# First norm of a two-layer decoder kernel: weight and shift applied behind the transposes

## The chip, the cores and the metric

The kernel runs on one core of one Trainium2 chip. The metric is the device time of one execution in microseconds (us). Engines: PE is TensorE (matmuls and transposes), DVE is VectorE, ACT is ScalarE, POOL is GpSimd, SP is SyncE, which here only issues DMAs. Each engine runs its instructions in order and waits for others by semaphores.

## The reference

Input x is 512 tokens of 2048 channels, float32. Layer 0 is a state-space mixer, layer 1 sparse attention with 16 heads; behind each a norm of the residual sum:

```
y = s5_mixer(x, ...)                       # layer 0, ends in "@ w_out" (1024 x 2048)
x1 = layer_norm(alpha * x + y, g0, b0)     # (v - mean) * rsqrt(var + eps) * g0 + b0
shared = shared_kv(x1, ...)                # x1 @ kv_w, block compression of K and V
y = nsa_mixer(x1, w_in, w_out, shared)     # x1 @ w_in: queries, gates
out = layer_norm(alpha * x1 + y, g1, b1)
```

Mean and variance run over the 2048 channels of a token; g and b are vectors over the channels. x1 has two uses: transposed (channels on the partitions) as an operand of all of layer 1's projections, and as it is, in the residual sum at the very end.

## The kernel before

A float32 product is made of three fp32r matmuls (`mm3`, L233 to L237): every operand is kept as a high part h, rounded by a copy on ACT, and a low part l, the difference, made by DVE. Below, a "product" is one such triple. Weights come in units of 128 x 1024: `Weights` loads a unit by SP (L56), splits it on ACT (L78) and DVE, or POOL for the units in `pool_units` (L85), two units ahead of use; `ahead(i)` forces the splits up to unit i. Split units lie in three buffers ("hl"); `W.extra` gives some units another pool and tag.

`project_out` (L904) does the last projection of a layer, the residual sum and the norm. Tokens lie on the partitions: four token tiles t of 128, four channel stretches cc of 512. The last of its four steps goes tile by tile, eight products a tile, and at each tile's end `done` adds the residual into v (L951), takes statistics (L952) and starts `finish(t)`. `finish` is a generator: it issues a piece of the norm of its tile, yields a number, and `Background.tick` continues it when that many ticks have gone by; a full product counts 3 ticks, a half product of layer 1's first tiles 1.5, so 21 ticks are 7 and 14 products. Its pieces stand in the engines' queues between the products of the next tiles. Lanes are served in the order of the tiles, and per tick one or two are continued.

For the first norm (`turn` is true) `finish` takes mean and variance (L962) and the root (L964, ACT), then subtracts the mean and multiplies with g (L970, DVE) for some stretches, makes the inverse of the root (L975 to L980), and then, by the letters in `LN_HOW`, multiplies with it and adds b: "d" on DVE (L983), "m" on ACT and POOL (L985, L986), "p" wholly on ACT and POOL (L988 to L990). The tile is then stored to x1_d for the residual (L1004, SP) and turned: four transposes per stretch on PE into a PSUM tile tp (two buffers, L1010), a copy from it to the high part (ACT, L1012), a subtraction from it to the low part (DVE, L1014). The low part reads tp, so tp is free only behind it.

After the last tile come the first two projection tiles of layer 1 (unit u1 to u1+3, split on POOL), in two halves of 256 tokens, 32 half products each: half 0 needs tiles 0 and 1 turned, half 1 tiles 2 and 3. `layer1_in` does the rest: its products tick a second `Background`, which holds the compression of K and V and the attention heads. POOL has, in the order of issue, small loads (`pos`, `w2`, L1181, L1185) and a memset of `ct` (L1240) that the compression waits for on ACT; its last small projection, `p`, is on PE. Before the first head, `bg.drain()` runs all that is left in the background, and the memory of this phase's pool is given to the heads.

The lines around the change:

Of the kernel before, what the change touches and what calls it, by code (L numbers as in the profile page):

```python
# [21 lines left out]
D = 2048  # L22
KD = D // 128
# [9 lines left out]
LN_EPS = 1e-5  # L33
# [130 lines left out]
def emit(tc, A, out):  # L164
# [34 lines left out]
    with ExitStack() as top:  # L199
        const = top.enter_context(tc.tile_pool(name="const", reuse_waits="tile", bufs=1))  # L200
        wp = top.enter_context(tc.tile_pool(name="wp", reuse_waits="tile", bufs=1))
        xp = top.enter_context(tc.tile_pool(name="xp", reuse_waits="tile", bufs=1))
        dram = top.enter_context(tc.tile_pool(name="dram", bufs=1, space=DRAM))
        W = Weights(nc, wp, units)
        W.by_dma.update(range(DMA_FROM, index["w_glu", 0]))
        c = Core(tc, A, W, index, const, xp)
        c.scope, c.dram = top, dram
        sz_d = dram.tile([KE, 128, T], F32, name="sz_d")
        x1_d = dram.tile([4, 128, D], F32, name="x1_d")
        y_d = dram.tile([NH, 128, T], F32, name="y_d")  # L210

        with ExitStack() as sc:
            yh, yl, yscope = layer0_in(c, sc, sz_d)
        with yscope, ExitStack() as sc:
            xh, xl = project_out(c, sc, index["w_out"], OUT0, KE, yh, yl, lambda k: None, A["x"], A["ln_g"][0],
                                 A["ln_b"][0], x1_d, True)
        with ExitStack() as sc:
            y = layer1_in(c, sc, seq, xh, xl, y_d)
# [685 lines left out]
def project_out(c, sc, u0, steps, K, yh, yl, prep, x_res, ln_g, ln_b, x_out, turn):  # L904
# [10 lines left out]
    n_u = K // 2  # L915
# [43 lines left out]
    fg = FG[turn]  # L959

    def finish(t):
# [3 lines left out]
        vs, gs, bs = ([z[:, cc * 512:cc * 512 + 512] for cc in range(4)] for z in (v[:, t], gb, bb))  # L965
        how = LN_HOW[turn][t]
        late = []
        early = [cc for cc in range(4) if how[cc] != "p"]
        for i, cc in enumerate(early):
            V.scalar_tensor_tensor(vs[cc], vs[cc], mv[:, t, 0:1], gs[cc], OP.subtract, OP.mult)  # L970
            if i % 2:
                yield fg[0]
            if i == (len(early) - 1 if turn else 1):

                V.reciprocal(r, r)  # L975
                V.tensor_scalar(q, mv[:, t, 1:2], LN_EPS, r, OP.add, OP.mult)
                V.tensor_scalar(q, q, r, -0.5, OP.mult, OP.mult)
                V.tensor_scalar(r, q, 1.5, r, OP.add, OP.mult)
                if "p" in how:
                    V.tensor_scalar(nb, mv[:, t, 0:1], r, -1.0, OP.mult, OP.mult)  # L980
        for cc in sorted(range(4), key=lambda cc: "pmd".index(how[cc])):
            if how[cc] == "d":
                V.scalar_tensor_tensor(vs[cc], vs[cc], r, bs[cc], OP.mult, OP.add)  # L983
            elif how[cc] == "m":
                S.activation(vs[cc], vs[cc], AF.Copy, scale=r)  # L985
                P.tensor_tensor(vs[cc], vs[cc], bs[cc], OP.add)  # L986
            else:
                S.activation(vs[cc], vs[cc], AF.Identity, scale=r, bias=nb)  # L988
                P.tensor_tensor(vs[cc], vs[cc], gs[cc], OP.mult)
                P.tensor_tensor(vs[cc], vs[cc], bs[cc], OP.add)  # L990
            if not turn:
                o = x_out[t, :, cc * 512:cc * 512 + 512]
                if how[cc] == "d":
                    SP.dma_start(o, vs[cc])
                elif POUT:
                    P.dma_start(o, vs[cc])
                else:
                    late.append((o, vs[cc]))
            yield fg[1]
        if not turn:  # L1000
            for o, z in late:
                SP.dma_start(o, z)
            return
        SP.dma_start(x_out[t], v[:, t])  # L1004
        yield fg[2]
        ts = slice(t * 128, t * 128 + 128)
        for cc in range(4):
            tp = pt.tile([128, 4, 128], F32, name="tp")
            for i in range(4):
                PE.transpose(tp[:, i], vs[cc][:, i * 128:i * 128 + 128], ident)  # L1010
            h, l = (z[:, 4 * cc:4 * cc + 4, ts] for z in (xh, xl))
            S.copy(h, tp)  # L1012
            yield fg[3]
            V.tensor_tensor(l, tp, h.bitcast(F32), OP.subtract)  # L1014
            turned[t] += 1

    bg = Background(4, True)

    def done(cc, t, ps):
        add(cc, t, ps)  # L1020
        if cc == 3:
            bg.add(t, finish(t))
            bg.advance(t)

    for step, (cc, tiles) in enumerate(steps):
# [55 lines left out]
POUT = 0

FG = {True: (9, 1, 9, 6), False: (4, 3)}

LN_HOW = {True: ('pddp', 'dppd', 'mdmm', 'dmmm'), False: ('dddd', 'dddd', 'dddd', 'dddd')}
# [395 lines left out]
SCALE = 128.0 ** -0.5  # L1481


def layer1_in(c, sc, seq, xh, xl, y_d):
# [170 lines left out]
```

## Time and profile before

| | |
|---|---|
| median of 3 runs | 1802.88 us (1795.56 to 1807.08) |
| profiled execution | 1799.01 us, span 1797.0 us |
| PE busy | 1742.9 us, 97% of the span |
| DVE busy | 1005.1 us, 56% |
| ACT busy | 607.3 us, 34% |
| POOL busy | 177.5 us, 10% |
| chain that ended last | PE 81%, DVE 3%, ACT 1% |
| mean granted clock of PE | 0.993 |

The profile is of one execution, whose own time stands beside its span; the runs of the table are others. Busy time is that of an engine's instructions; where PE is busy throughout, the other engines' work lies beside it and costs nothing. The chain is followed back from the last instruction, at each step to what released it. [...]

### The profile page before, as it was taken

The numbers are of one execution on the slowest core, as the hardware profiler recorded it, in microseconds if no ns is written. First come the engines' busy times: TensorE is split into PE (matmuls) and PEld (weight loads), VectorE is DVE, ScalarE is ACT, GpSimd is POOL, SyncE is SP. The second block draws the span as 40 slices with busy tenths as digits, with TensorE's granted clock in tenths as the row PEclk, the third lists the DMA queues.
The fourth block names the chain that finished last, engine by engine and source line by source line (L and its number), as shares of the span: only waits on it lengthen the run. The fifth ranks groups of instructions, "written<-read, shape, count | busy, mean of one in ns | idle before, by whom it ended". The sixth has DMA issues, their size and how long they took to land.

```text
span 1797.0 us, 21851 instructions
## 1 busy us (share of the span) xinstructions
PE 1742.9 (97%) x8455; PEld 1446.2 (80%) x8455; DVE 1005.1 (56%) x1817; ACT 607.3 (34%) x1020; POOL 177.5 (10%) x233
## 2 busy tenths in 40 slices
PE   8799999997999999999999999999999999999997
PEld 6678887886788888888888888888888888888886
DVE  7678866458233455653555553555543555665346
ACT  3344435324333333332323332333332333333120
POOL 4911100006000000000000000000000000010000
PEclk9999999999999999999999999999999999999999
DMA  6587874543233322222222222222222222236343
GB/s 226 139 198 195 215 173 146 192 148 141 83 118 117 106 83 77 82 83 83 89 78 81 88 79 92 88 76 88 76 84 94 88 77 82 77 129 232 120 140 105
DMA packets 89751, 209.70 MB, mean 117 GB/s; under 512 B 25264, under 2 KB 34720, under 8 KB 88624
## 3 DMA queue, kind: packets, MB, share of 16 engines
q1 hardware_dynamic: 81008, 181.31, 30.5%
q0 software_dynamic: 6336, 22.81, 5.2%
q10 hardware_dynamic: 2304, 4.20, 0.6%
q8 instruction: 66, 1.08, 0.2%
q14 instruction: 37, 0.30, 0.0%
HBM read 188.42 MB, written 19.86 MB: 116 GB/s over the span
## 4 chain that ended last, share of the span: by engine, by line
PE 81%; DVE 3%; ACT 1%; issue 0%; DMA 0%; POOL 0%; SPq 0%; DVEq 0%; POOLq 0%; ACTq 0%
PE ps L235 23%; PE ps L237 23%; PE ps L236 23%; PE tp L1459 2%; PE s L237 1%; PE s L235 1%; PE s L236 1%; PE o L236 1%; PE o L237 1%; DVE v L970 1%; PE o L235 1%; PE cps L1224 1%; PE tp L1424 0%; PE tp L1010 0%; DMA z<-sz_d 0%
## 5 line engine op out<-in xcount | busy, mean ns | idle before, releaser
L235 PE MATMUL ps<-x1h,hl 128*128 128x512 f32 (+1 forms) x1440 | 564.8, 392 | 1.6 <-ACT hl L78 1.6
L237 PE MATMUL ps<-x1h,hl 128*128 128x512 f32 (+1 forms) x1440 | 557.9, 387 | 0.5 <-DVE hl L85 0.5
L236 PE MATMUL ps<-x1l,hl 128*128 128x512 f32 (+1 forms) x1440 | 556.8, 387 | 0.0
L85 DVE TENSOR_TENSOR hl<-wr,hl 128x1024 fp32r<-128x1024 f32 (+1 forms) x247 | 300.9, 1222 | 311.3 <-ACT hl L78 307.4
L78 ACT CAST hl<-wr 128x1024 fp32r<-128x1024 f32 (+1 forms) x273 | 284.4, 1045 | 223.3 <-PE ps L237 183.6
L237 PEld LDWEIGHTS ps<-x1h,hl 128*128 128x128 f32 x1440 | 271.4, 189 | 57.3 <-DVE hl L85 1.0
L235 PEld LDWEIGHTS ps<-x1h,hl 128*128 128x128 f32 x1440 | 272.0, 189 | 48.5 <-ACT hl L78 1.8
L236 PEld LDWEIGHTS ps<-x1l,hl 128*128 128x128 f32 x1440 | 271.9, 189 | 46.6
L1396 ACT ACTIVATE p<-s,m 128x384 f32<-128x384 f32 (+3 forms) x128 | 67.7, 529 | 357.9 <-DVE m L1395 357.9
L1332 POOL TENSOR_TENSOR y<-y,z 128x512 f32<-128x512 f32 x32 | 41.5, 1298 | 999.8 <-DVE z L1331 863.0
L241 DVE TENSOR_TENSOR pl<-tp,ph 128x512 fp32r<-128x512 f32 (+3 forms) x128 | 61.9, 487 | 109.7 <-ACT ph L240 109.4
L237 PE MATMUL ps<-xh,hl 128*128 128x512 f32 x256 | 102.9, 402 | 12.6 <-DMA hl<-w_in_b 12.6
L235 PE MATMUL ps<-xh,hl 128*128 128x512 f32 x256 | 107.9, 422 | 5.6 <-ACT xh L788 5.6
L240 ACT CAST ph<-tp 128x512 fp32r<-128x512 f32 (+3 forms) x128 | 54.2, 427 | 150.8 <-PE tp L1459 150.6
L236 PE MATMUL ps<-xl,hl 128*128 128x512 f32 x256 | 102.4, 400 | 2.3 <-DVE xl L789 2.3
L235 PE MATMUL ps<-hl,y1h 128*128 128x512 f32 x256 | 99.7, 389 | 0.0
L237 PE MATMUL ps<-hl,y1l 128*128 128x512 f32 x256 | 99.6, 389 | 0.0
L236 PE MATMUL ps<-hl,y1h 128*128 128x512 f32 x256 | 99.6, 389 | 0.0
L237 PEld LDWEIGHTS ps<-xh,hl 128*128 128x128 f32 x256 | 49.3, 192 | 24.6 <-DMA hl<-w_in_b 13.9
L1395 DVE TENSOR_REDUCE m<-s 128x1 f32<-128x384 f32 (+3 forms) x128 | 62.8, 491 | 4.4
L1318 DVE SCALAR_TENSOR_TENSOR z<-z,ps 128x512 f32<-128x512 f32 x48 | 33.0, 687 | 57.2 <-ACT z L1317 57.1
L235 PEld LDWEIGHTS ps<-xh,hl 128*128 128x128 f32 x256 | 49.4, 193 | 15.7 <-ACT xh L788 5.6
(350 smaller groups left out, 2306.3 us busy)
## 6 DMA issues: line engine op xcount, KB each, us to landing
wr<-b_w_in SPq DMA_DIRECT2D x128, 512.0 KB, 3.2
wr<-kv_w SPq DMA_DIRECT2D x48, 512.0 KB, 3.2
wr<-b_w_out SPq DMA_DIRECT2D x32, 512.0 KB, 3.5
wr<-w_in_b SPq DMA_DIRECT2D x24, 512.0 KB, 5.0
hl<-w_in_b POOLq DMA_DIRECT2D x22, 512.0 KB, 7.3
wr<-w_out SPq DMA_DIRECT2D x16, 512.0 KB, 3.4
xr<-xT SPq DMA_DIRECT2D x16, 256.0 KB, 4.4
Tz<-k_d SPq DMA_DIRECT2D x64, 64.0 KB, 4.9
```

Of the source, the lines that this page charges most:

```text
L78: self.nc.scalar.copy(h[:, :n], r[:, :n])
L85: eng.tensor_tensor(l[:, :n], r[:, :n], h[:, :n].bitcast(F32), OP.subtract)
L235: PE.matmul(o, sh, mh, start=start, stop=False)
L236: PE.matmul(o, sh, ml, start=False, stop=False)
L237: PE.matmul(o, sl, mh, start=False, stop=stop)
L240: self.nc.scalar.copy(h, src)
L241: self.nc.vector.tensor_tensor(l, src, h.bitcast(F32), OP.subtract)
L1318: self.nc.vector.scalar_tensor_tensor(z, z, 1.0, ps, OP.add, OP.mult)
L1332: P.tensor_tensor(y[0], y[0], z, OP.add)
L1395: self.nc.vector.tensor_reduce(m[:, b - 1, i:i + 1], s, AX.X, OP.max, negate=True)
L1396: self.nc.scalar.activation(self.p[h, b][i], s, AF.Exp, bias=m[:, b - 1, i:i + 1], accum_out=self.sums[h, b][:, i:i + 1])
L1459: PE.transpose(tp[:, 128 * (i - j):128 * (i - j) + 128], p[i][:, at:at + 128], ident)
```

## The change

For the first norm a new `finish_turn` replaces `finish`. It only subtracts the mean and multiplies with the inverse root: stretches 0 and 2 on DVE, 1 and 3 on ACT (`LN_ACT`). 21 ticks later it begins to turn: transposes; then each 128 x 128 block is multiplied with g and shifted by b on its way out of PSUM into a new tile x in SBUF, by a weight and a shift per partition (gbT, one small load), blocks 0 and 2 on ACT, 1 and 3 on DVE (`XT_ACT`); ACT's copy to the high part and DVE's subtraction then read x. The stretches follow at 6 ticks. The stored tile is now the norm without weight and shift (xn_d), and a new generator `residual` makes x1_d from it in layer 1, on POOL alone: sixteen chunks, each a load, a multiplication, an addition and a store. Unit u1+1 gets a buffer of its own and is split at the end of tile 2; u1+2 and u1+3 take the two buffers that u1+1 and u1+2 had. The second norm keeps its instructions. `inverse` holds the four instructions L975 to L978; the last line of the diff stands in `layer1_in`, behind the first `kc_tiles`.

```diff
         if turn:
-            W.extra[u1 + 1 + i] = (st, "x", 2)
-    gb = st.tile([128, D], F32, name="gb")
-    bb = st.tile([128, D], F32, name="bb")
-    P.dma_start(gb, ln_g.partition_broadcast(128))
-    P.dma_start(bb, ln_b.partition_broadcast(128))
+            W.extra[u1 + 2 + i] = (st, "x", 2)
+            W.extra[u1 + 1] = (st, "w", 1)
+    if turn:
+        gbT = st.tile([128, 2, KD], F32, name="gbT")
+        P.dma_start(gbT, c.A["ln0"])
...
+    def finish_turn(t):
         V.bn_aggr(mv[:, t], stats[:, t])
         r, q, nb = (rs[:, t, i:i + 1] for i in range(3))
         S.activation(r, mv[:, t, 1:2], AF.Sqrt, bias=eps)
+        inverse(t)
+        V.tensor_scalar(nb, mv[:, t, 0:1], r, -1.0, OP.mult, OP.mult)
+        vs = [v[:, t, cc * 512:cc * 512 + 512] for cc in range(4)]
+        ts = slice(t * 128, t * 128 + 128)
+        for cc in range(4):
+            if LN_ACT[cc]:
+                S.activation(vs[cc], vs[cc], AF.Identity, scale=r, bias=nb)
+            else:
+                V.tensor_scalar(vs[cc], vs[cc], mv[:, t, 0:1], r, OP.subtract, OP.mult)
+        yield TG[0]
         for cc in range(4):
             tp = pt.tile([128, 4, 128], F32, name="tp")
             for i in range(4):
                 PE.transpose(tp[:, i], vs[cc][:, i * 128:i * 128 + 128], ident)
+            x = st.tile([128, 4, 128], F32, tag="xt", name="xt", bufs=3)
+            for i in range(4):
+                g, b = (gbT[:, j, 4 * cc + i:4 * cc + i + 1] for j in range(2))
+                if i in XT_ACT:
+                    S.activation(x[:, i], tp[:, i], AF.Identity, scale=g, bias=b)
+                else:
+                    V.tensor_scalar(x[:, i], tp[:, i], g, b, OP.mult, OP.add)
             h, l = (z[:, 4 * cc:4 * cc + 4, ts] for z in (xh, xl))
-            S.copy(h, tp)
-            yield fg[3]
-            V.tensor_tensor(l, tp, h.bitcast(F32), OP.subtract)
+            S.copy(h, x)
+            yield TG[1]
+            V.tensor_tensor(l, x, h.bitcast(F32), OP.subtract)
             turned[t] += 1
+        SP.dma_start(x_out[t], v[:, t])
...
-                if t == 3 and turn:
-                    W.ahead(u1 + i)
+                if turn and (t == 3 or (t, i) == (2, n_u - 1)):
+                    W.ahead(u1 + i if t == 3 else u1 + 1)
...
+TG = (21, 6)
...
+LN_ACT = (0, 1, 0, 1)
+XT_ACT = (0, 2)
...
+def residual(c, pool, xn_d, x1_d):
+    P = c.nc.gpsimd
+    for half in range(2):
+        g, b = (pool.tile([128, 1024], F32, tag=n, name=n) for n in ("g0", "b0"))
+        hs = slice(half * 1024, half * 1024 + 1024)
+        P.dma_start(g, c.A["ln_g"][0][hs].partition_broadcast(128))
+        P.dma_start(b, c.A["ln_b"][0][hs].partition_broadcast(128))
+        for t in range(4):
+            for i in range(2):
+                cs, here = (slice(lo, lo + 512) for lo in (half * 1024 + i * 512, i * 512))
+                x = pool.tile([128, 512], F32, tag="xn", name="xn", bufs=2)
+                P.dma_start(x, xn_d[t, :, cs])
+                yield RGAP
+                P.tensor_tensor(x, x, g[:, here], OP.mult)
+                P.tensor_tensor(x, x, b[:, here], OP.add)
+                P.dma_start(x1_d[t, :, cs], x)
+                yield RGAP
...
+RGAP = 18
...
+    bg.add(3, residual(c, cp, xn_d, x1_d))
```

## Rows read from the trace of the kernel before

**Rows 1.** Groups by line, 399.5 to 449 us: count, busy us, mean ns, idle before, releasers.

```profile
L970 DVE SCALAR_TENSOR_TENSOR v<-v,mv,gb 128x512 f32<-128x512 f32 x12 | 17.4, 1491 | 0.1
...
L1014 DVE TENSOR_TENSOR x1l<-tp,x1h 128x512 fp32r<-128x512 f32 x16 | 10.8, 685 | 5.7 <-ACT x1h L1012 5.6
L85 POOL TENSOR_TENSOR hl<-wr,hl 128x1024 fp32r<-128x1024 f32 x4 | 10.7, 2675 | 0.8 <-ACT hl L78 0.8
L1010 PE MATMUL tp<-ident,v 128*128 128x128 f32 x64 | 10.3, 285 | 9.2 <-DVE x1l L1014 3.4 <-DVE v L983 2.6 <-DVE rs L975 2.0
...
L983 DVE SCALAR_TENSOR_TENSOR v<-v,rs,bb 128x512 f32<-128x512 f32 x6 | 5.0, 854 | 0.0
...
L78 ACT CAST hl<-wr 128x1024 fp32r<-128x1024 f32 x4 | 4.2, 1040 | 0.0
```

**Rows 2.** Stretches: length, busy time (instructions) of PE, PEld, DVE, ACT, POOL, clock, DMA share, GB/s.

```profile
406.50:437.00 30.50, 21.29 (x135) 17.86 (x134) 29.70 (x42) 13.46 (x22) 25.68 (x14) 1.00 0.37 129
437.00:458.50 21.50, 21.40 (x167) 21.01 (x165) 5.61 (x10) 6.00 (x11) 7.01 (x12) 0.92 0.28 111
...
465.30:608.00 142.70, 142.70 (x709) 118.87 (x708) 49.67 (x58) 46.04 (x60) 0.57 (x3) 1.00 0.35 115
```

**Rows 3.** PE in order of time: start, duration in us, line, shapes, count.

```profile
438.51 0.41 PE L236 MATMUL ps<-x1l,hl 128*128 128x256 f32 x1
...
446.65 0.36 PE L235 MATMUL ps<-x1h,hl 128*128 128x256 f32 x1
...
458.12 0.28 PE L237 MATMUL ps<-x1h,hl 128*128 128x256 f32 x1
```

**Rows 4.** DVE in order of time, first tile of the norm and last subtraction.

```profile
399.55 0.69 DVE L951 SCALAR_TENSOR_TENSOR v<-xr,ps 128x512 f32<-128x512 f32 x1 [1.95 <-PE ps L237]
...
401.30 1.42 DVE L970 SCALAR_TENSOR_TENSOR v<-v,mv,gb 128x512 f32<-128x512 f32 x2
...
403.57 0.21 DVE L980 TENSOR_SCALAR rs<-mv,rs 128x1 f32<-128x1 f32 x1
...
405.17 0.69 DVE L951 SCALAR_TENSOR_TENSOR v<-xr,ps 128x512 f32<-128x512 f32 x1
...
446.94 1.30 DVE L1014 TENSOR_TENSOR x1l<-tp,x1h 128x512 fp32r<-128x512 f32 x2 [0.82 <-ACT x1h L1012]
```

**Rows 5.** Groups by line and shape over the whole span, ACT and DVE.

```profile
L240 ACT CAST ph<-tp 128x128 fp32r<-128x128 f32 x32 | 8.6, 269 | 36.4 <-PE tp L1459 36.4
...
L240 ACT CAST yh<-sig 128x512 fp32r<-128x512 f32 x8 | 5.0, 620 | 11.3 <-DVE sig L893 11.3
...
L1380 DVE TENSOR_TENSOR s<-s,causal 128x128 f32<-128x128 f32 x64 | 19.0, 297 | 11.6 <-PE s L237 10.5
...
L1448 DVE TENSOR_SCALAR p<-p,r 128x512 f32<-128x512 f32 x32 | 15.4, 480 | 0.0
...
L241 DVE TENSOR_TENSOR yl<-sig,yh 128x512 fp32r<-128x512 f32 x8 | 5.5, 693 | 5.5 <-ACT yh L240 5.5
```

**Rows 6.** Groups by line and shape over the whole span, POOL.

```profile
L1332 POOL TENSOR_TENSOR y<-y,z 128x512 f32<-128x512 f32 x32 | 41.5, 1298 | 999.8 <-DVE z L1331 863.0 <-DVE pc L1378 136.7
...
L1335 POOL DMA_DIRECT2D y_d<-y x16 | 9.0, 560 | 4.8 <-POOL y L1332 4.5 <-DMA yr<-y_d 0.3
```

**Rows 7.** DMA issues: queue, count, size of one, median us from issue to landing.

```profile
raw<-bc POOLq DMA_DIRECT2D x8, 256.0 KB, 7.6
...
y_d<-y POOLq DMA_DIRECT2D x16, 256.0 KB, 2.3
...
xr<-x_d SPq DMA_DIRECT2D x16, 256.0 KB, 3.3
...
bb<-ln_b POOLq DMA_DIRECT2D x2, 1024.0 KB, 10.7
```

**Rows 8.** PE's instructions on tile p: duration min/median/max ns, first and last start.

```profile
L235 PE MATMUL p<-w2h,cth x4: 221/248/250, 606.8 to 607.6; 128*96 128x128 f32 x4
```

**Rows 9.** Line L970 over the whole span: duration min/median/max ns, first and last start.

```profile
L970 DVE SCALAR_TENSOR_TENSOR v<-v,mv,gb x28: 737/746/2865, 401.3 to 1789.9; 128x512 f32<-128x512 f32 x28
```

More of the change, by code (lines that the diff above doesn't have):

```diff
@@ L210, in emit @@
         y_d = dram.tile([NH, 128, T], F32, name="y_d")
+        xn_d = dram.tile([4, 128, D], F32, name="xn_d")
         with ExitStack() as sc:
@@ L215, in emit @@
             xh, xl = project_out(c, sc, index["w_out"], OUT0, KE, yh, yl, lambda k: None, A["x"], A["ln_g"][0],
-                                 A["ln_b"][0], x1_d, True)
+                                 A["ln_b"][0], xn_d, True)
         with ExitStack() as sc:
-            y = layer1_in(c, sc, seq, xh, xl, y_d)
+            y = layer1_in(c, sc, seq, xh, xl, y_d, xn_d, x1_d)
         with ExitStack() as sc:
@@ L921, in project_out @@
         if turn:
-            W.extra[u1 + 1 + i] = (st, "x", 2)
-    gb = st.tile([128, D], F32, name="gb")
-    bb = st.tile([128, D], F32, name="bb")
-    P.dma_start(gb, ln_g.partition_broadcast(128))
-    P.dma_start(bb, ln_b.partition_broadcast(128))
+            W.extra[u1 + 2 + i] = (st, "x", 2)
[4 more added lines that the diff above has]
+    else:
+        gb = st.tile([128, D], F32, name="gb")
+        bb = st.tile([128, D], F32, name="bb")
+        P.dma_start(gb, ln_g.partition_broadcast(128))
+        P.dma_start(bb, ln_b.partition_broadcast(128))
     v = st.tile([128, 4, D], F32, name="v")
@@ L958, in project_out, with inverse @@
     turned = [0] * 4
-    fg = FG[turn]
-    def finish(t):
+    def inverse(t):
+        r, q = rs[:, t, 0:1], rs[:, t, 1:2]
+        V.reciprocal(r, r)
+        V.tensor_scalar(q, mv[:, t, 1:2], LN_EPS, r, OP.add, OP.mult)
+        V.tensor_scalar(q, q, r, -0.5, OP.mult, OP.mult)
+        V.tensor_scalar(r, q, 1.5, r, OP.add, OP.mult)
+    def finish_turn(t):
         V.bn_aggr(mv[:, t], stats[:, t])
@@ L964, in finish @@
         S.activation(r, mv[:, t, 1:2], AF.Sqrt, bias=eps)
[L965 to L986, printed above, removed]
-            else:
[L988 to L1006, printed above, removed]
+        inverse(t)
[5 more added lines that the diff above has]
+                S.activation(vs[cc], vs[cc], AF.Identity, scale=r, bias=nb)
+            else:
+                V.tensor_scalar(vs[cc], vs[cc], mv[:, t, 0:1], r, OP.subtract, OP.mult)
@@ L1010, in finish @@
                 PE.transpose(tp[:, i], vs[cc][:, i * 128:i * 128 + 128], ident)
+            x = st.tile([128, 4, 128], F32, tag="xt", name="xt", bufs=3)
[5 more added lines that the diff above has]
+                    V.tensor_scalar(x[:, i], tp[:, i], g, b, OP.mult, OP.add)
             h, l = (z[:, 4 * cc:4 * cc + 4, ts] for z in (xh, xl))
-            S.copy(h, tp)
-            yield fg[3]
-            V.tensor_tensor(l, tp, h.bitcast(F32), OP.subtract)
+            S.copy(h, x)
+            yield TG[1]
+            V.tensor_tensor(l, x, h.bitcast(F32), OP.subtract)
             turned[t] += 1
+        SP.dma_start(x_out[t], v[:, t])
+    def finish(t):
+        V.bn_aggr(mv[:, t], stats[:, t])
+        r = rs[:, t, 0:1]
+        S.activation(r, mv[:, t, 1:2], AF.Sqrt, bias=eps)
+        vs, gs, bs = ([z[:, cc * 512:cc * 512 + 512] for cc in range(4)] for z in (v[:, t], gb, bb))
+        for cc in range(4):
+            V.scalar_tensor_tensor(vs[cc], vs[cc], mv[:, t, 0:1], gs[cc], OP.subtract, OP.mult)
+            if cc % 2:
+                yield FG[0]
+            if cc == 1:
+                inverse(t)
+        for cc in range(4):
+            V.scalar_tensor_tensor(vs[cc], vs[cc], r, bs[cc], OP.mult, OP.add)
+            SP.dma_start(x_out[t, :, cc * 512:cc * 512 + 512], vs[cc])
+            yield FG[1]
     bg = Background(4, True)
@@ L1021, in done @@
         if cc == 3:
-            bg.add(t, finish(t))
+            bg.add(t, (finish_turn if turn else finish)(t))
             bg.advance(t)
@@ L1078, in project_out @@
     return xh, xl
[L1081 to L1085 removed]
+FG = (4, 3)
+TG = (21, 6)
+LN_ACT = (0, 1, 0, 1)
+XT_ACT = (0, 2)
 OPOOL = (0, 1, 2, 3)
@@ L1481, with layer1_in @@
 SCALE = 128.0 ** -0.5
-def layer1_in(c, sc, seq, xh, xl, y_d):
+def residual(c, pool, xn_d, x1_d):
[16 more added lines that the diff above has]
+RGAP = 18
+def layer1_in(c, sc, seq, xh, xl, y_d, xn_d, x1_d):
     tc, nc, A, W, index, mm3, split = c.tc, c.nc, c.A, c.W, c.index, c.mm3, c.split
@@ L1631, in layout @@
         "ln_g": ln_g,
+        "ln0": np.stack([a[0].reshape(KD, 128).T for a in (ln_g, ln_b)], 1),
         "ln_b": ln_b,
```

3 lines of the change are left out of this document (2 added, 1 removed).

## The prediction

> **What bounds the kernel now.** I read the page first: TensorE (PE) is busy in nearly the whole span and carries most of the chain of waits, so an edit pays only where PE stands still or runs slow. The groups by line, around the end of the first norm, name the place: its transposes (L1010) wait 9.2 us in all, most of it for the subtraction on VectorE (DVE) that releases a transpose's PSUM buffer and for DVE's norm [rows 1]. The table by stretches shows why. From 406.5 to 437 us DVE is busy 29.7 of 30.5 us, PE only 21.3: this stage is DVE's. [...] From 465.3 to 608 us PE never stops; there the change can only cost.
>
> **The ledger of DVE, for that is what must get shorter.** Before, first instruction of the norm at 399.55, last subtraction done at 446.94 + 1.30 = 448.24: 48.7 us for four token tiles [rows 4].
>
> Removed from DVE: twelve subtract-and-weight passes (L970), 17.4 us, and six shift passes (L983), 5.0 us [rows 1]. Removed from GpSimd (POOL): fourteen tensor operations (L986, L989, L990). Removed are also the two broadcast loads of 1 MB, at 327 us, where nothing waits for them: zero. SP's stores of v no longer wait for the norm with weight loads behind them; PE does not wait for a load there, so zero too.
>
> Added on DVE: eight tensor_scalar passes from SBUF at 0.48, 3.8 us; thirty-two 128x128 scale-and-shift passes out of PSUM, for which no row exists; the nearest is DVE's 128x128 add on PSUM, 0.30, and from below the same less the 0.08 by which two that don't depend on each other overlap (two L970, of 0.75 each, in 1.42 [rows 4]). I take 0.30, 9.6 us. The sixteen subtractions stay, 0.69 each [rows 5]. On busy time DVE wins 22.4 - 13.4 = 9 us.
>
> But the change also lengthens what DVE waits for, since engines run in order. (a) Before, the passes L970 ran while ScalarE (ACT) took the square root. Now the reciprocal follows the statistics at once and waits for the root. Per tile: 399.55 to 403.78 less the two passes (1.42), plus 0.5 for the root, is 3.3 us, and two tensor_scalars make it 4.3 us [rows 4, 5]. (b) Per 512 columns the way is now: two passes of DVE (0.60), then ACT's copy from SBUF (0.62), then DVE's subtraction (0.69) [rows 5]; each needs the one before, and nothing of another tile stands between them in DVE's queue for most of the run. That is 1.9 us, four times 7.6 us per tile. (c) The split of u1 and u1+1 is now issued ahead of tile 2's root: two ACT halves of 1.04, 2.1 us [rows 1], which the root, the reciprocal and all behind them wait for. Sum: 4 x (4.3 + 7.6) + 2.1 = 49.7 us, against 48.7. The 9 us are spent on hand-overs.
>
> Where PE meets this: a transpose is in PE's queue and needs one of two PSUM buffers, now released by the scale-and-shift passes. Tile 1's fourth transposes need the buffer of its second, whose passes stand in DVE's queue behind tile 2's whole statistics and norm, 4.3 + 2.1 us, while PE has about four products ahead of it, 4 x 0.70 = 2.8 us (eight products from one L951 at 399.55 to the next at 405.17) [rows 4], and two sets of transposes, some 0.9. One wait of about 3 us there, a like one for tile 2 behind tile 3's norm, and about 1.5 us at tile 0's fourth: 7 to 9 us, against 9.2. [...]
>
> Best value: the chain starts at 399.55, ends near 449, and after tile 3's last subtraction PE has at least 20 half products left, 20 x 0.367 (half 1 runs from 446.65 to 458.4 for 32) = 7.3 us, so half 1 can end at 456.5 instead of 458.4 [rows 3, 4]. **Turn: -2 us.** From below: that overlap of 0.08, over ten such pairs a tile, is 3 us more: -5. From above +1.5, see the third rival.
>
> ACT: thirty-two passes of 0.27 are added, 8.6 us [rows 5]; two of ten long passes go. It is DVE's chain that waits for ACT, not ACT's work that is too much. POOL's four weight splits (2.68 each) stay [rows 1] and are no longer behind norm work; they are due when half 0 starts and its second n: zero. The own buffer for u1+1 only moves a split earlier; its price is (c).
>
> **The moved work: weight, shift and x1_d in layer 1.** Thirty-six DMAs and thirty-two tensor operations go onto POOL's queue from about 459 us. A chunk is: issue 0.56, landing, two operations of 1.3, issue of the store 0.56 [rows 6]. The landing of 256 KB on this queue is bounded by 2.3 (y_d's store) and 7.6 (raw, at the start), the nearest by stretch and direction is xr from x_d, 3.3 [rows 7]: chunk 7.0 us, between 6.0 and 11.3. The traffic is 10 MB in 130 us, on DMA engines that are 0.35 busy there [rows 2]; weights land in 3 us and are asked for two units ahead: zero. At the drain before attention, two steps are left and issued at once; the pool's memory is handed on, and DVE and ACT may wait some us behind it with two weight units in hand: 0, at most 5.
>
> Sum against the profiled run (span 1797.0, own time 1799.0): -2 gives 1797. The median of the runs shown is 1802.9, 3.9 above that run; forecast **1801 us**.
>
> **Rivals.**
> *All waits go* (20%). DVE's 9 us show up, because at 1.9 us per 512 columns it keeps pace with two products and a transpose on PE (1.8 us), and PSUM buffers come free earlier than before, after the passes and not after the subtraction. For it: POOL's fourteen operations, which held DVE up, are gone. Against it: (a) and (c). [...]
>
> *POOL falls behind* (8%), the one that makes it slower. The chunks are paced in the program, but POOL waits for no product, only for its own loads, one at a time; and the memset of ct and the load of pos stand in the same queue. The second memset comes after 14 chunks and two broadcast loads (10.7 for 1 MB, so up to 7.4 beyond a chunk's own landing): 459 + 15 + 14c, with c the time of a chunk. ACT needs it before PE's p at 606.8 [rows 7, 8]; with 1.5 us between, c must stay under 9.3. At 7.0 POOL is there at 572, so it costs nothing. At the upper bound, 11.3, it is there at 632 and PE stands some 27 us: 1830. From c = 10.7 it is over 18 us.
>
> *POOL's remaining splits hit DVE* (14%). L970, with two operands in SBUF, took up to 2.87 us where 0.75 is usual, and only while POOL worked: 17.4 - 12 x 0.746 = 8.5 us lost in a stretch with 25.7 us of POOL [rows 1, 2, 9]. L1014, with one operand in PSUM, averaged 0.685 throughout [rows 1]. Now its second operand lies in SBUF as well. At 8.5/25.7 = 0.33 us per us of POOL, the four splits (10.7 us) cost 3.5 us, net +1.5; if every microsecond of them held DVE, 10.7, net +9. Time 1804 to 1812, say 1806.
> [...]
>
> The remaining 2% is for anything else. The forecast itself has 56%, its own range 1795 to 1806.
>
> **Range and chances.** What a measurement of this kernel can tell from no change is about 1%, 18 us; three runs of one kernel lie 11.5 us apart. 1789 to 1809 takes in the full gain, the measured contention and part of the full lock; POOL falling behind and the rest of the lock stay outside. Faster by over 1% (under 1785) would need more than the turn has to give: 4%. Slower by over 1% (over 1821) needs POOL behind: 8%. Within 1%: 88%.
>
> **What would show it.** Right: L970's place taken by short passes, DVE busy in the turn falling by some 9 us but with idle time behind ACT's copy; two waits of transposes over 2.5 us, at tile 1's and tile 2's last; half 1 ending between 453 and 460; PE full from 465 to 608. The step on the hand-overs is wrong if DVE's cycle per 512 columns is well under 1.8 us or the waits sum to under 4 us. POOL's chunk is read from the distance of two stores; over 9.3 us, and an ACT that waits for ct, means the second rival. If subtractions of over 1 us stand beside splits, it is the third.

## The result, and the profile after

The changed kernel takes 1813.15 us (median of 11 runs, 1809.7 to 1818.54) against 1802.88 before: ratio 1.0069 [1.0055, 1.0082]. **It is 0.7% slower, and 4 us above the range forecast.** The profiled execution took 1809.78 us with a span of 1807.9, 10.9 more than before.

All of it is in the turn. Three stretches of the kernel after (length, busy time of PE, PEld, DVE, ACT, POOL, clock, DMA share, GB/s):

```profile
406.50:437.00 30.50, 18.76 (x89) 14.43 (x88) 19.70 (x43) 17.38 (x32) 5.39 (x3) 0.83 0.13 46
437.00:458.50 21.50, 15.90 (x118) 15.08 (x117) 13.29 (x30) 12.30 (x24) 4.24 (x2) 0.92 0.50 196
475.00:618.00 143.00, 143.00 (x702) 118.87 (x701) 58.76 (x59) 46.59 (x61) 65.19 (x68) 1.00 0.56 174
```

In the first stretch DVE is busy 19.7 us of 30.5, where it was full before [rows 2], and PE does less as well, 18.8 against 21.3. No engine is full: that is how a chain of hand-overs looks in such a table. DVE's work is not gone, it is spread over a longer turn. From DVE's first addition to its last subtraction, before and after (same columns):

```profile
399.50:448.30 48.80, 39.59 (x247) 34.29 (x246) 41.92 (x64) 20.64 (x34) 31.41 (x18) 0.97 0.40 144
```
```profile
399.20:462.10 62.90, 45.56 (x270) 39.05 (x269) 39.55 (x88) 34.01 (x64) 9.63 (x4) 0.89 0.30 114
```

DVE is busy 41.9 us before and 39.6 after: 2.4 us less, not the 9 that were forecast. Layer 1, in the last line, is full on PE as before, though POOL now works 65 us there. What PE waited for in the turn (from 395 to 475 us: us in total, times, longest), and single waits of its transposes (in brackets) with one matmul behind the longest:

```profile
PE tp L995 <- DVE xt L1002: 17.3, 9, 6.7
```
```profile
412.95 0.66 PE L995 MATMUL tp<-ident,v 128*128 128x128 f32 x4 [3.33 <-DVE xt L1002]
...
429.61 1.12 PE L995 MATMUL tp<-ident,v 128*128 128x128 f32 x4 [6.68 <-DVE xt L1002]
...
430.95 0.63 PE L238 MATMUL ps<-hl,yh 128*128 128x512 f32 x1
...
444.85 0.66 PE L995 MATMUL tp<-ident,v 128*128 128x128 f32 x4 [4.54 <-DVE xt L1002]
```

17.3 us of waits instead of 9.2 [rows 1]: 8.1 of the 10.9. Behind the long wait a 512-column matmul took 0.63 us where 0.39 to 0.40 is usual in this stretch: the granted clock was 0.50 from 425.0 to 435.2 us, as it was in the kernel before from 438.1 to 441.4. That is the rest: from DVE's first addition to the second copy `first<-ps` PE is busy 52.8 us at a mean granted clock of 0.90, where it was busy 49.6 us at 0.97 before: 3.2 us more for the same matmuls. The order of DVE and of ACT in one stretch of 512 columns shows why the waits grew (start, duration):

```profile
399.26 0.69 DVE L960 SCALAR_TENSOR_TENSOR v<-xr,ps 128x512 f32<-128x512 f32 x1 [1.87 <-PE ps L239]
...
401.34 0.16 DVE L972 RECIPROCAL rs<-rs 128x1 f32<-128x1 f32 x1 [0.36 <-ACT rs L981]
...
402.42 0.99 DVE L990 TENSOR_SCALAR v<-v,mv,rs 128x512 f32<-128x512 f32 x2
...
416.22 0.69 DVE L1006 TENSOR_TENSOR x1l<-xt,x1h 128x512 fp32r<-128x512 f32 x1 [0.69 <-ACT x1h L1004]
416.83 0.41 DVE L1002 TENSOR_SCALAR xt<-tp,gbT 128x128 f32<-128x128 f32 x1
417.77 0.41 DVE L1002 TENSOR_SCALAR xt<-tp,gbT 128x128 f32<-128x128 f32 x1 [0.53 <-ACT xt L1000]
418.87 0.69 DVE L1006 TENSOR_TENSOR x1l<-xt,x1h 128x512 fp32r<-128x512 f32 x1 [0.69 <-ACT x1h L1004]
...
423.59 0.16 DVE L972 RECIPROCAL rs<-rs 128x1 f32<-128x1 f32 x1 [1.16 <-ACT rs L981]
...
424.67 3.02 DVE L990 TENSOR_SCALAR v<-v,mv,rs 128x512 f32<-128x512 f32 x2
...
461.33 0.69 DVE L1006 TENSOR_TENSOR x1l<-xt,x1h 128x512 fp32r<-128x512 f32 x1 [0.69 <-ACT x1h L1004]
```
```profile
416.10 0.45 ACT L1000 ACTIVATE xt<-tp,gbT 128x128 f32<-128x128 f32 x1
417.27 0.46 ACT L1000 ACTIVATE xt<-tp,gbT 128x128 f32<-128x128 f32 x1 [0.73 <-DVE xt L1002]
418.21 0.62 ACT L1004 CAST x1h<-xt 128x512 fp32r<-128x512 f32 x1 [0.48 <-DVE xt L1002]
...
469.46 0.59 ACT L1086 COPY first<-ps 128x512 f32<-128x512 f32 x1 [5.17 <-PE ps L239]
```

Read the two fences together by start. The four blocks of a stretch do not run two and two at the same time: ACT 416.10, DVE 416.83, ACT 417.27, DVE 417.77. The last two are each released by the block before them on the other engine, though no block needs another's data; a release is a semaphore, so it is the program that keeps this order. ACT's first block (416.10) lies beside the subtraction of the stretch before (416.22), its second stands in the chain. Then come ACT's copy and DVE's subtraction: 2.65 us from one subtraction to the next. The last subtraction ends at 462.02; the chain from DVE's first addition at 399.26 is 62.8 us long (48.7 before), and the last copy of the two halves starts at 469.46 instead of 458.44.

DVE's groups in the turn (count, busy us, mean ns, idle us before and its releaser) sum it up: 20 us of DVE's idle time stand ahead of blocks and subtractions.

```profile
L1002 DVE TENSOR_SCALAR xt<-tp,gbT 128x128 f32<-128x128 f32 x32 | 13.1, 408 | 11.2 <-ACT xt L1000 11.2
L1006 DVE TENSOR_TENSOR x1l<-xt,x1h 128x512 fp32r<-128x512 f32 x16 | 11.0, 690 | 8.9 <-ACT x1h L1004 8.9
L990 DVE TENSOR_SCALAR v<-v,mv,rs 128x512 f32<-128x512 f32 x8 | 6.7, 881 | 0.0
```

POOL in order of time: the two splits ahead of tile 2's norm, the first three stores of the moved work, and its second memset of ct:

```profile
422.50 4.90 POOL L85 TENSOR_TENSOR hl<-wr,hl 128x1024 fp32r<-128x1024 f32 x2 [93.25 <-DVE mv L979]
...
479.81 0.59 POOL L1511 DMA_DIRECT2D x_d<-xn  x1 [0.30 <-POOL xn L1510]
...
487.78 0.57 POOL L1511 DMA_DIRECT2D x_d<-xn  x1 [0.30 <-POOL xn L1510]
...
497.48 0.57 POOL L1511 DMA_DIRECT2D x_d<-xn  x1 [0.30 <-POOL xn L1510]
...
607.94 0.23 POOL L1251 MEMSET ct<- 128x128 f32 x1
```

A chunk takes 8 to 10 us, not 7.0, and PE never waits for it.

### The profile page after: what moved, and what is told of

It is laid out like the page before. It is cut to its first block, busy times and chain, and to the rows that moved or that the text cites. A ratio compares the mean times of both kernels' runs of the same rounds, so it can differ in the third digit from the quotient of the medians.

```text
span 1807.9 us, 21958 instructions
## 1 busy us (share of the span) xinstructions
PE 1748.7 (97%) x8455; PEld 1450.0 (80%) x8455; DVE 1011.1 (56%) x1841; ACT 620.8 (34%) x1050; POOL 224.5 (12%) x286
## 4 chain that ended last, share of the span: by engine, by line
PE 80%; DVE 3%; ACT 2%; issue 0%; DMA 0%; SPq 0%; DVEq 0%; ACTq 0%
PE ps L237 23%; PE ps L239 23%; PE ps L238 23%; PE tp L1470 2%; PE s L239 1%; PE s L237 1%; PE s L238 1%; PE o L238 1%; PE o L239 1%; PE o L237 1%; PE cps L1235 1%; DVE xt L1002 1%; ACT xt L1000 0%; DVE x1l L1006 0%; PE tp L1435 0%
## 5 line engine op out<-in xcount | busy, mean ns | idle before, releaser
L85 DVE TENSOR_TENSOR hl<-wr,hl 128x1024 fp32r<-128x1024 f32 (+1 forms) x247 | 306.2, 1244 | 304.1 <-ACT hl L78 300.2
L237 PEld LDWEIGHTS ps<-x1h,hl 128*128 128x128 f32 x1440 | 271.9, 189 | 48.7 <-ACT hl L78 1.8
L239 PEld LDWEIGHTS ps<-xh,hl 128*128 128x128 f32 x256 | 49.7, 194 | 23.5 <-DMA hl<-w_in_b 12.4
```

Of the source, the lines that this page charges most:

```text
L85: eng.tensor_tensor(l[:, :n], r[:, :n], h[:, :n].bitcast(F32), OP.subtract)
L237: PE.matmul(o, sh, mh, start=start, stop=False)
L239: PE.matmul(o, sl, mh, start=False, stop=stop)
```

## The experiments

The measure that separates them best is the **turn**, read from each profile: from DVE's first addition of tile 0 in the last step to the start of the second copy `first<-ps`. One execution gives it, and what the clock did in layer 0 (from 200 to 399 us it was granted at 1.00 in the kernel after and at 0.97 in e4_both; the profiled executions differ there by up to 8 us) is not in it. In the last four rows PE waits 1.7 us more ahead of the turn, added here. The column of waits has the sum of the transposes' waits. Where the expectations count 18 or 21 "products" (TG), ticks are meant, that is single matmuls, three to a product.

| kernel | turn, us | against before | waits, us | ratio to before | median, us |
|---|---|---|---|---|---|
| before | 58.9 | | 9.2 | | 1802.88 |
| after | 70.2 | +11.3 | 17.3 | 1.0069 [1.0055, 1.0082] | 1813.15 |
| e1_stretch | 65.4 | +6.5 | 13.6 | 1.0043 [1.0028, 1.0059] | 1810.69 |
| e2_act | 61.5 | +2.6 | 9.4 | 1.0010 [0.9997, 1.0023] | 1802.55 |
| e3_order | 67.8 | +8.9 | 13.6 | 1.0045 [1.0028, 1.0061] | 1807.98 |
| e4_both | 58.0 | -0.9 | 8.8 | 0.9992 [0.9980, 1.0005] | 1801.10 |
| e5_banks | 65.9 | +7.0 | 12.0 | 1.0043 [1.0029, 1.0058] | 1808.80 |
| e6_late | 60.3 | +1.4 | 10.0 | 1.0014 [1.0000, 1.0027] | 1802.56 |
| e7_act | 59.9 | +1.0 | 9.1 | 1.0024 [1.0010, 1.0039] | 1804.40 |
| e8_nores | 70.2 | +11.3 | 16.6 | 1.0066 [1.0053, 1.0079] | 1812.27 |
| e9_early | 56.6 + 1.7 | -0.6 | 6.6 | 1.0003 [0.9989, 1.0017] | 1799.77 |
| e10_pool | 56.6 + 1.7 | -0.6 | 7.5 | 1.0012 [0.9998, 1.0027] | 1802.44 |
| e11_pool18 | 54.5 + 1.7 | -2.7 | 7.0 | 0.9981 [0.9970, 0.9993] | 1798.29 |
| e12_18 | 61.3 + 1.7 | +4.1 | 9.4 | 1.0028 [1.0010, 1.0046] | 1805.74 |

Kernels were compared with runs of before on their own chip, so ratios count more than medians. 0.001 is 1.8 us; apart from e7_act and e10_pool the turn and the ratio agree within 1.2 us.

**e1_stretch: one engine for all blocks of a stretch.**

```diff
-                if i in XT_ACT:
+                if cc in XT_ACT:
```

> The changed kernel with one edit: the four weight-and-shift blocks of a 512-column stretch are all on ACT (stretches 0 and 2) or all on DVE (1 and 3), in place of taking turns within a stretch. Theory (one PSUM bank is read by ACT and DVE one after the other, so the blocks of a stretch form a chain ACT, DVE, ACT, DVE): no block waits for the other engine any more; a pair of stretches takes about 4 x 0.37 + 0.62 + 0.69 + 4 x 0.33 + 0.62 = 4.7 us instead of 2 x 2.64, so the turn is some 4 us shorter, time about 1809. Rival (the chain is the hand-overs root, copy, subtraction and the queue order, whoever does the blocks): within 1 us of the changed kernel's 1813. Rival (GpSimd's splits hold DVE's tensor_scalars): also 1813.

Measured 1810.69, the turn 4.8 us shorter than after: near the theory's 1809 and 4 us, and outside the rivals' 1 us around 1813. Waits 13.6 us. Four blocks in a row, 1.50 us on ACT and 1.36 on DVE, do not hand over.

**e2_act: all blocks on ACT.**

```diff
-XT_ACT = (0, 2)
+XT_ACT = (0, 1, 2, 3)
```

> The changed kernel with one edit: all sixteen-by-four weight-and-shift blocks on ACT, none on DVE. Theory (turns between two engines on one bank): ACT does the blocks of a stretch and its copy in 4 x 0.37 + 0.53 = 2.0 us, DVE's subtraction runs beside the next stretch's blocks, and a PSUM buffer is no longer released behind the next tile's norm on DVE; 0.6 us x 16 = 10 us shorter, time about 1803, although ACT gets twice its blocks. Rival (DVE's hand-overs root and copy are the cost): 4 us at most. Rival (ACT becomes the bound with root, normal passes, weight halves and 64 blocks): slower than 1813.

Measured 1802.55, waits 9.4. ACT does twice as many blocks as in the kernel after, and the time falls by 10 us, so the loss was not ACT's work. What it was this run alone doesn't separate: the edit takes away the turn-taking, and with it DVE's blocks and their place in DVE's queue behind the next tile's norm.

**e3_order: the subtraction behind the next stretch's blocks**, so that it doesn't stand on DVE's queue waiting for ACT's copy; blocks alternate as in after.

```diff
+            if cc:
+                V.tensor_tensor(l, xp, h.bitcast(F32), OP.subtract)
+                turned[t] += 1
             h, l = (z[:, 4 * cc:4 * cc + 4, ts] for z in (xh, xl))
             S.copy(h, x)
+            xp = x
             yield TG[1]
-            V.tensor_tensor(l, x, h.bitcast(F32), OP.subtract)
-            turned[t] += 1
+        V.tensor_tensor(l, xp, h.bitcast(F32), OP.subtract)
+        turned[t] += 1
```

> The changed kernel with one edit: DVE's subtraction of a stretch is issued behind the next stretch's blocks instead of ahead of them; the blocks still take turns between ACT and DVE. Theory: the chain of four blocks and ACT's copy stays (0.46 + 0.41 + 0.46 + 0.41 + 0.53, some 2.3 us), only the subtraction (0.6) leaves it, partly: 0.3 x 16 = 5 us shorter, time about 1808. Rival (the hand-over copy to subtraction is all of it): over 10 us shorter, 1803 or less.

Measured 1807.98, as expected. The cycle falls only to 2.40 us (subtractions at 414.22, 416.62 and 419.01): the alternating blocks and ACT's copy fill it.

**e4_both: e1 and e3 together.**

> Both edits: blocks of a stretch all on one engine, and the subtraction issued behind the next stretch's blocks. Theory: ACT's and DVE's shares of two stretches run beside each other, 2.5 us per pair on each (4 x 0.37 + 2 x 0.53, 4 x 0.33 + 2 x 0.61), half of the 5.3 us measured; the turn is then PE's but for the norms between the tiles, waits of transposes fall from 17 to under 8 us, time 1793 to 1800, at or under the kernel before. Rival (queue order: transposes wait behind the next tile's statistics whatever the cycle is): the waits stay over 12 us and the time over 1805.

Measured 1801.10, level with before, a microsecond above the range expected. Here ACT and DVE work on different stretches at the same time. What is left, PE's transposes and DVE in order of time:

```profile
417.06 0.66 PE L995 MATMUL tp<-ident,v 128*128 128x128 f32 x4 [1.17 <-DVE xt L1002]
...
429.94 1.12 PE L995 MATMUL tp<-ident,v 128*128 128x128 f32 x4 [5.11 <-DVE xt L1002]
...
441.88 0.66 PE L995 MATMUL tp<-ident,v 128*128 128x128 f32 x4 [2.52 <-DVE xt L1002]
```
```profile
424.50 0.17 DVE L972 RECIPROCAL rs<-rs 128x1 f32<-128x1 f32 x1 [1.83 <-ACT rs L981]
...
425.58 3.02 DVE L990 TENSOR_SCALAR v<-v,mv,rs 128x512 f32<-128x512 f32 x2
428.53 1.35 DVE L1002 TENSOR_SCALAR xt<-tp,gbT 128x128 f32<-128x128 f32 x4
```

The 5.11 us are tile 1's transposes, whose buffer waits for blocks (428.53) that stand in DVE's queue behind tile 2's root (waited for 1.83 us where 0.36 is usual, since two splits stand ahead of it on ACT) and behind two passes that took 3.02 us beside POOL's splits, where an undisturbed pair takes 0.99.

**e5_banks: ACT's and DVE's blocks in two PSUM tiles.**

```diff
-            tp = pt.tile([128, 4, 128], F32, name="tp")
+            tps = [pt.tile([128, 2, 128], F32, tag=f"tp{z}", name="tp", bufs=1) for z in "ad"]
+            tp = [tps[i % 2][:, i // 2] for i in range(4)]
```

> After with one edit: the four 128x128 blocks of a stretch of 512 columns lie in two PSUM tiles, each in a bank of its own, ScalarE's two blocks in one and VectorE's two in the other; each tile has one buffer instead of two, so the transposes of the next stretch must wait until both engines have read this one. Theory (the two engines take turns because their blocks share a PSUM bank): ScalarE's and VectorE's blocks start together, within 0.2 us, and the four blocks of a stretch take about 0.95 us instead of 1.74; the cycle from one subtraction to the next falls from 2.64 to about 1.9 us, by which the turn would gain up to 11 us of the kernel after, less what TensorE waits for the single buffers (0.9 us of reading for each stretch that comes right behind another): about 1803 us, 1798 to 1811. Rival (they take turns for the shared tile in SBUF that both write, or for another reason): the blocks still alternate, 1.74 us for four, and with one buffer fewer the time is 1813 or more.

The blocks now overlap, two on ACT and two on DVE, in the same microsecond:

```profile
410.43 0.81 ACT L1001 ACTIVATE xt<-tp,gbT 128x128 f32<-128x128 f32 x2 [0.44 <-PE tp L996]
```
```profile
410.54 0.73 DVE L1003 TENSOR_SCALAR xt<-tp,gbT 128x128 f32<-128x128 f32 x2 [1.20 <-PE tp L996]
...
417.40 0.69 DVE L1007 TENSOR_TENSOR x1l<-xt,x1h 128x512 fp32r<-128x512 f32 x1 [0.77 <-ACT x1h L1005]
418.01 0.72 DVE L1003 TENSOR_SCALAR xt<-tp,gbT 128x128 f32<-128x128 f32 x2
419.47 0.69 DVE L1007 TENSOR_TENSOR x1l<-xt,x1h 128x512 fp32r<-128x512 f32 x1 [0.74 <-ACT x1h L1005]
```

Same engines, same order, same tile x; what differs is that each engine reads a PSUM tile of its own. **The alternation comes from the PSUM tile that both engines read.** The rival, the shared tile x, falls. Two tiles in one bank were not tried, so the runs don't say whether the order is kept by the tile or by the bank. Where PE doesn't hold it up, the cycle is 2.07 us (417.40 to 419.47) instead of 2.64: the turn-taking is worth 0.57 us of it. The time, 1808.80, is in the range but far from the 1803 expected: with one buffer each PE waits 12.0 us, 10.1 of them for ACT's blocks. The edit shortens the turn by 4.3 us only; the rest of what it gains goes into these waits.

**e6_late: u1+1 split behind tile 2's root** (on e4_both, which its text calls the last experiment but one).

```diff
-                if turn and (t == 3 or (t, i) == (2, n_u - 1)):
-                    W.ahead(u1 + i if t == 3 else u1 + 1)
+                if turn and t == 3:
+                    W.ahead(u1 + max(i, 1))
```

> The kernel of the last experiment but one (all four blocks of a stretch on one engine, and the subtraction behind the next stretch's blocks), with one more edit: the unit u1+1 is split behind token tile 2's last product and its root, not ahead of it. In that kernel's trace the root of tile 2 stood behind two casts of 1 us (VectorE idle for 1.83 us) and the pair of scale-and-shift passes behind it took 3.02 us beside GpSimd's two splits, where an undisturbed pair takes 0.99; the wait of the transposes at tile 1's last was 5.1 us. Theory (that wait is the rest of the loss, and the queue's order makes it): the root comes about 1 to 2 us earlier, the pair takes about 1 us, the wait at tile 1's last falls to 1.5 to 3 us, and the time is 1797 to 1800, ratio to before 0.997 to 0.999. Rival (the splits only move onto tile 3's norm): the wait at tile 2's last grows from 2.5 by as much, and the time is that of the kernel without the edit, 1801.

The theory missed. Root and pair came back to normal (the root waited for 0.36 us, the pair 0.99), but POOL's splits now met two subtractions (DVE, then POOL):

```profile
431.22 2.31 DVE L1004 TENSOR_TENSOR x1l<-xt,x1h 128x512 fp32r<-128x512 f32 x1 [1.98 <-ACT x1h L1008]
433.46 2.90 DVE L1010 TENSOR_TENSOR x1l<-xt,x1h 128x512 fp32r<-128x512 f32 x1
```
```profile
428.28 10.28 POOL L85 TENSOR_TENSOR hl<-wr,hl 128x1024 fp32r<-128x1024 f32 x4 [92.56 <-ACT hl L78]
```

0.69 us became 2.31 and 2.90, and the longest wait, 5.4 us, moved to tile 2's last. The rival was right: the same loss at another tile.

**e7_act: e6_late with the whole norm pass on ACT.**

```diff
-LN_ACT = (0, 1, 0, 1)
+LN_ACT = (1, 1, 1, 1)
```

> The kernel of e6_late with one more edit: all four scale-and-shift passes of a tile's norm on ScalarE instead of two on each engine, so that VectorE has no pass in SBUF alone that GpSimd's splits stretch. Theory (what is left of the waits is VectorE's queue): VectorE is free right behind the short operations of the norm and takes the waiting blocks 1 to 3 us earlier, the waits fall to 3 to 5 us, 1795 to 1799 us. Rival (ScalarE becomes the bound: 3.0 us of passes in a row stand ahead of its copies and blocks): the waits, now released by ScalarE, are 7 us or more and the time is 1801 or above.

Waits 9.1 us, now 5.0 for ACT and 4.1 for DVE, 1804.40: the rival. The wait went to the other engine.

**e8_nores: without the moved work.**

```diff
-                                 A["ln_b"][0], xn_d, True)
+                                 A["ln_b"][0], x1_d, True)
...
-    bg.add(3, residual(c, cp, xn_d, x1_d))
```

> After without the work that the change moved to GpSimd in layer 1: the turn stores the normalised rows straight into the residual, and the weight and the shift are left out of the residual that the last norm adds (those rows are computed without them). Theory (the 11 us are all lost in the turn; the moved work lies beside TensorE's full stretches): 1812 to 1814 us, within 0.1% of the kernel after. Rival (the loads, passes and stores in layer 1 cost some of it): 1803 to 1810.

1812.27, within 0.1% of after. From 475 to 618 us:

```profile
475.00:618.00 143.00, 143.00 (x700) 118.91 (x699) 52.10 (x60) 47.52 (x62) 0.56 (x3) 1.00 0.35 116
```

PE is full with and without 65 us of POOL and with DMA at 0.56 or 0.35. The moved work costs nothing that can be measured.

**e9_early: the splits of u1 and u1+1 ahead of tile 0's products** (on e4_both).

```diff
             hl = [W.get(us + i, n_u - 1 - i) for i in range(n_u)]
+            if turn:
+                W.ahead(u1 + 1)
...
-                if turn and (t == 3 or (t, i) == (2, n_u - 1)):
-                    W.ahead(u1 + i if t == 3 else u1 + 1)
+                if turn and t == 3:
+                    W.ahead(u1 + i)
```

> The kernel with both edits (all four blocks of a stretch on one engine, the subtraction behind the next stretch's blocks), with one more: the units u1 and u1+1 are split right behind the last step's weights, ahead of token tile 0's first product, instead of ahead of tile 2's root; u1+2 and u1+3 stay beside tile 3. Where these splits stood ahead of the root, VectorE's pair of scale-and-shift passes took 3.02 us instead of 0.99; where they were put behind it, two subtractions took 2.31 and 2.90 us instead of 0.69 and the waits did not fall. Theory (GpSimd's splits cost VectorE wherever they meet it, so they must run where VectorE has nothing to do in SBUF): GpSimd's first two splits run beside tile 0's products, no VectorE pass of tile 2 is stretched, the waits of the transposes fall from 8.8 to 4 to 6 us, and the time is 1796 to 1799, ratio to before 0.997 to 0.999. Rival (TensorE is held by the sum of VectorE's own work, not by the splits): waits of 8 us or more, and 1801 or above.

Waits of the transposes 6.6 us, a little over the theory's 4 to 6, but time level at 1.0003. The pair of tile 2 is undisturbed (1.00); the longest wait, 3.9 us, is at tile 2's last, behind tile 3's root, for which DVE now waits 1.83 us, since splits stand ahead of it on ACT. POOL's split now ran beside DVE's last two splits of the step (DVE, then POOL):

```profile
394.98 4.40 DVE L85 TENSOR_TENSOR hl<-wr,hl 128x1024 fp32r<-128x1024 f32 x2
```
```profile
394.79 2.38 POOL L85 TENSOR_TENSOR hl<-wr,hl 128x1024 fp32r<-128x1024 f32 x1 [65.54 <-ACT hl L78]
```

4.40 us instead of 2.34, and PE waited 1.7 us for these weights, which it had not done. Gained at one place, paid at another.

**e10_pool: e9_early with the low parts of two stretches a tile on POOL.**

```diff
-                V.tensor_tensor(l, xp, h.bitcast(F32), OP.subtract)
+                (P if cc in LO_POOL else V).tensor_tensor(l, xp, h.bitcast(F32), OP.subtract)
```

> The kernel of e9_early with one more edit: the low parts of a tile's first two stretches are subtracted on GpSimd instead of VectorE (8 of 16 passes of 0.69 us). Theory (VectorE's sum is the bound: 9.1 us of work for each token tile against 7.1 us of TensorE's): VectorE's work in the turn falls by 5.5 us, the waits to 1 to 4 us, 1793 to 1797 us. Rival (GpSimd in SBUF beside VectorE in SBUF stretches what is left on VectorE, as the splits did): the tensor_scalar pairs take 1.7 to 3 us, the waits are no shorter than in e9_early, and the time is its own or up to 6 us above.

The rival's numbers: eight passes, 5.5 us of work, less on DVE, and the waits did not fall (7.5 against 6.6), nor did the time, 1802.44. Its reason holds for one pair of four, tile 3's, which took 2.81 us beside POOL (1.86 in e9_early). The other waits, 1.2 and 1.6 us, are those of e9_early: the buffer that a fourth stretch's transposes need is released by blocks behind the next tile's norm in DVE's queue, and the sum of DVE's work is not the bound there.

**e11_pool18: e10_pool, turning begun three ticks earlier**, and the early splits one unit later.

```diff
-TG = (21, 6)
+TG = (18, 6)
...
-            if turn:
-                W.ahead(u1 + 1)
...
-                if turn and t == 3:
-                    W.ahead(u1 + i)
+                if turn and (t == 3 or (t, i) == (0, 0)):
+                    W.ahead(u1 + (i if t else 1))
```

> The kernel of e10_pool (half of the low parts on GpSimd) with two more edits: the first transposes of a tile 18 instead of 21 products behind it, so that the second stretch's blocks are queued on VectorE ahead of the next tile's statistics and norm instead of behind them; and the early splits of u1 and u1+1 one unit of tile 0's products later, off the two last-step splits that took 4.40 us instead of 2.34 and held TensorE for 1.7 us. Theory (in e9_early and e10_pool the transposes of a third stretch wait for the second stretch's blocks, which stand behind the next tile's norm in VectorE's queue): those waits (1.2, 1.6 and 3.9 to 4.7 us) fall to 0 to 1.5 us each, the 1.7 us go, and the time is 1794 to 1798. Rival (the norm isn't ready after 18 products, 4.2 us, and VectorE's lag against TensorE grows with each tile whatever the order): waits of 6 us or more move to the first stretch of a tile, 1799 to 1803.

1798.29, ratio 0.9981 [0.9970, 0.9993]: faster than before and after, by 0.2% and 0.9%. The reason given holds in half. PE's waits, two lines of the view:

```profile
PE tp L995 <- ACT xt L1000: 7.0, 3, 2.5
PE ps L238 <- DVE hl L85: 1.7, 1, 1.7
```

The transposes no longer wait for DVE, and no wait is longer than 2.5 us. But the waits sum to 7.0, over the rival's 6, and stand where the rival put them, at the first stretch of tiles 1, 2 and 3; and the 1.7 us stayed. The turn came down by 2.1 us, the sum of the waits only by 0.5. The rest is the clock: the 328 matmuls of the turn kept PE busy for 47.5 us at a granted clock of 1.00, in e10_pool for 49.0 at 0.97.

**e12_18: the same on e9_early**, all low parts on DVE.

> The same two edits on the kernel of e9_early, with all low parts on VectorE. Theory (queue order): waits of 2 to 4 us and 1795 to 1798. Rival (VectorE's 9.1 us of work for a tile against 7.1 us of TensorE's: the lag grows by 2 us a tile): waits of 6 us or more, 1799 to 1802, and e11_pool18 is faster than this one by 1 to 4 us.

1805.74: the rival, and worse than it. Waits 9.4 us, and DVE's lag grows: its additions of tiles 1, 2 and 3 come 0.6, 2.1 and 5.5 us later behind tile 0's than in e11_pool18. With all subtractions on DVE the earlier turn costs 4.7 us more than the later one (e9_early), with half of them on POOL it gains 2.1. So the earlier turn pays only with less work on DVE for a tile, and less work alone paid nothing (e10_pool).

## Why the prediction was wrong

**The step that failed is (b)**, "two passes of DVE (0.60), then ACT's copy from SBUF (0.62), then DVE's subtraction (0.69)", 1.9 us per 512 columns. It let ACT's two blocks run beside DVE's. They take turns, and the second of ACT's stands in the chain: the measured cycle is 0.61 (subtraction) + 0.41 + 0.46 + 0.41 (blocks) + 0.62 (copy) and 0.13 of hand-overs, 2.64 us. Of the 0.74 above the forecast, 0.57 is the turn-taking (e5_banks without it: 2.07), and the remaining 0.17 goes with the dearer blocks. 16 times 0.74 is 11.8 us. With (a) at -0.6, (c) at -1.3 and POOL's splits at +2.8, all below, that makes 12.7 of the 13.1 us by which the chain, 62.8 us, came out longer than the forecast's 49.7. That the shared PSUM tile is the reason for the turns is shown by e5_banks. That the turn-taking with the order behind it is the loss is shown by e1_stretch, e3_order and e4_both: without either, e4_both takes 1801.10 us, with waits of 8.8 where 7 to 9 were foreseen. That this is the forecast's own number is in part luck, for its blocks have other prices and its subtraction has moved.

The traces show the blocks in order where both engines read one PSUM tile (at 417.77 in the kernel after DVE's second had waited 0.53 us for ACT's), and side by side where each has a tile of its own (0.81 us on ACT from 410.43, 0.73 on DVE from 410.54 in e5_banks). What happens in one tile without the order wasn't tried. The prediction counted no turns. With them, at its own prices, the step would have been 1.9 + 0.27 = 2.2 us with one of ACT's blocks beside the subtraction, as here, and 2.4 with none: an estimate from the sum in (b) and the 0.27 of [rows 5].

The block prices were low too: 0.41 on DVE and 0.46 on ACT for 0.30 and 0.27, taken from operations of the same size but another kind [rows 5]. That makes 13.1 us on DVE instead of 9.6; the norm's eight passes took 6.7 instead of 3.8, since POOL's splits met four of them. So of the 22.4 us taken off DVE 19.8 came back, and its work fell by 2.4 us, not by 9: the sign that the prediction names for itself failed here, before any hand-over.

**(a)** was right: 4.15 us from the first addition to the end of the norm in tile 0 (4.3 forecast), with the wait for the root inside it. **(c)** was over-sized: the reciprocal waited 1.16 us instead of 0.36, so 0.8, not 2.1, since DVE was itself late: its statistics ended at 422.43, a microsecond after ACT had begun the split at 421.38.

**The waits** stood where they were foreseen, at the fourth transposes of tiles 0, 1 and 2, and were 3.3, 6.7 and 4.5 us instead of 1.5, 3 and 3. Six smaller ones, of 0.6 us or less, were not foreseen. And the clock, for which the forecast has no term, cost 3.2 us more: PE was busy 52.8 us at 0.90, before 49.6 at 0.97.

**The third rival**, POOL's splits on DVE, was partly right and joined the loss: the first tensor_scalar pair beside a split took 3.02 us, another 1.71, together 2.8 over the undisturbed 0.99 (3.5 foreseen). It hit tensor_scalars; no subtraction of the kernel after met a split, while e6_late shows that they are hit as well. Blocks read from PSUM beside a split (436.82 and 437.76 in the kernel after) kept their 0.41. Of the terms in the prediction's range no run shows the full gain, since in none did all the waits go (6.6 us were left at the least, in e9_early), nor a full lock, DVE held for every microsecond of POOL's splits: in the kernel after the four splits took 9.6 us and cost DVE 2.8.

**Layer 1** was right: the moved work is free (e8_nores), though its chunk was mis-sized, 8 to 10 us for 7.0, since a load of 256 KB landed in 4.8 us where 3.3 was taken. The mean distance of the first eight stores was 8.9 us, so the second rival stayed out, but by 0.4 us under its threshold of 9.3.

## What to carry to other kernels

Before splitting a job between ScalarE and VectorE, ask whether both halves lie in one PSUM tile: here they then alternated with a hand-over each time (2.64 us a stretch, 2.07 with a tile for each engine), and giving each engine whole tiles was faster than giving each half of every tile (a turn of 65.4 us, e1_stretch, for 70.2). A price for a chain of engines is the distance of one instruction to its next repetition, with every block on it; work taken off an engine that waits won nothing here (5.5 us less on VectorE in e10_pool, and no less time). And ask where GpSimd's work meets VectorE's in SBUF: beside GpSimd's splits VectorE's passes took 3.02 us for 0.99 and its subtractions 2.31 and 2.90 for 0.69, while blocks that it read from PSUM kept their 0.41. Moving the work only moved the loss in three kernels here (e6_late, e7_act, e9_early).

## What the runs showed of the hardware that was not expected

- Four 128x128 blocks from PSUM take 1.36 us in a row on DVE and 1.50 on ACT (e1_stretch, e4_both); alternating between them, the four of tile 0's first stretch in the kernel after took 1.84, from ACT's start at 404.62 to DVE's end at 406.46.
- POOL seems to be held as well: the first multiplication of the moved work took 4.28 us (from 473.87), where 1.29 is usual, beside subtractions of DVE in SBUF from 473.69 to 476.99; a later one took 3.39 us (from 529.23), beside two such subtractions from 529.09 to 531.47.
- The same 328 matmuls of the turn kept PE busy for 47.5 us in e11_pool18, 49.0 in e10_pool and 50.0 in e9_early, at granted clocks of 1.00, 0.97 and 0.94. Their waits are alike, 7.0, 7.5 and 6.6 us, and the longest single ones 2.5, 4.7 and 3.9 us: e11_pool18, with no wait over 2.5 us, had 1.00 throughout, but between the other two the longest wait doesn't tell which has the lower clock.
